# An RWKV-7, neighbourhood-attention and FFN layer: the last merge block behind the last output, weight conversions behind ScalarE's carry copies, and three smaller reorderings

## The chip, the cores and the metric

The kernel runs on one core of one Trainium2 chip, in one launch. The metric is the device time of one execution in microseconds (us). The matrix products run on TensorE (PE, its weight loads PEld), elementwise work on VectorE (DVE) and ScalarE (ACT), some of it and some DMA issues on GpSimd (POOL), and most DMA issues on SyncE (SP). Each engine works through its own queue in order.

## The reference, cut to what matters

One layer is applied to 512 latent tokens and, with the same weights, to 128 context tokens; the kernel works on all 640 columns at once.

```python
def _trunk_layer(x, cvec, s0, ctx_k, ctx_v, p):
    sh1, sc1, g1, sh2, sc2, g2 = _modulation(cvec, p["w_ada"], p["b_ada"])
    h = _rmsnorm(x, p["norm1_g"]) * (1.0 + sc1) + sh1
    u_rw, u_na, gate_rw, gate_na = jnp.split(h @ p["w_in"], IN_SPLITS, axis=-1)
    o_rw, s_new = _rwkv_branch(u_rw, s0, ...)
    ...
    o_na = _na_context(q, k, v)      # or _na_latent(...)
    merged = (jax.nn.sigmoid(gate_rw) * (o_rw @ p["w_o_rwkv"])
              + jax.nn.sigmoid(gate_na) * (o_na @ p["w_o_na"]))
    x = x + g1 * (merged @ p["w_out"])
    h2 = _rmsnorm(x, p["norm2_g"]) * (1.0 + sc2) + sh2
    x = x + g2 * ((jax.nn.silu(h2 @ p["ffn_w1"]) * (h2 @ p["ffn_w3"])) @ p["ffn_w2"])
    return x, s_new, k, v
```

The RWKV branch has 8 heads of 64. The step that costs most is the scan `s = s*w + (s a) b + v k`, once forward and once backward over the tokens, with `k_bonus = 0.5*(k_dir[0] + k_dir[1])` entering the output through `sum(r * k_bonus * r_k) * v`.

## The kernel before, in words

**Products.** A weight or activation is held as two parts, `hi` (rounded) and `lo` (what is left), and a product is three matmuls: hi by hi, hi by lo, lo by hi (`feat_gen`, L220 to L233). A weight chunk comes by DMA as `wst`; `wcast` (L191) makes both parts: for some chunks ScalarE writes the negated copy (L197), a GpSimd DMA adds the chunk to it (L198) and ScalarE writes the `hi` part (L199); for the others ScalarE writes `hi` and VectorE subtracts (L202). An activation is split by `split` (ScalarE L218, VectorE L219).

**Stages.** Norm, modulation and the QKV products run until about 190 us, the attention until about 240 us. Then come four RWKV blocks, `ct` = 0 to 3, of two heads each, until about 621 us; then the last merge products and the output projection `w_out` until about 660 us; then the second norm and the FFN, to the end.

**One block.** `main` forms the products between the chunks' keys (the first are the matmuls of L1306 on `AG`, which VectorE fills at L1285; `R_` is filled at L1288). `inv` inverts triangular matrices on VectorE alone, from the transpose L1412 to the transposes L1462 and L1464, and TensorE's L1475 waits for them. `carry` then takes the states through eight steps, each a chain between engines: TensorE L1536 forms `px`, ScalarE copies it (`x0`, L1539), TensorE L1565 multiplies, ScalarE copies to `ZV` (L1571), TensorE L1578 multiplies, VectorE scales (L1590). During the carry, `prep` prepares the next block: small products (`lora`, L762 and L764) that ScalarE reads through activations (L767, L770), copies for a second small product (L791, read by TensorE at L796), powers and exponentials (L786, L819 to L838), and products on VectorE (L840 to L868). The last of them, L868, adds the two directions into `bv`, which the bonus product reads later (L1268). `out` normalises the block's result and splits it (`yo`).

**What fills TensorE meanwhile.** A generator `stream` runs the large projections and merge products, in the units that the table `order` lists: `l`, `k`, `r`, `v` and `g` for projections, `a0` to `a3` for the attention part of the merge product, `b0` to `b3` for its RWKV part. Between the steps of the block's own work it issues some of these matmuls into two PSUM tiles (`fl`). Work that other engines do on a finished product (the copies L657 to L663 and the shifts L668 to L671 of a projection, the gates of a merge product, the conversion of a weight) is put off by `later` with a due time counted in TensorE's steps, and with a cost (ScalarE's and VectorE's share in us); a weight's conversion has the cost (1.05, 0). `tick` lets what is due run. In the carry, `beside(gen, budget)` fills each of a step's slots with due work and with steps of `prep` until a budget is used up. Slot 1 stands in front of L1536, slot 2 in front of `x0` and slot 3 behind the `ZV` copies.

**The end of the RWKV stage.** Merge unit `b<i>` covers output tiles `c8` = 2i and 2i + 1, each in two halves of 320 columns. Nine matmuls a half take the three finished blocks (a tile of `o` each). VectorE then multiplies the product by the gate (L1708, tile `mx`) and adds it to `mt` (L1710): eight instructions for a unit. The fourth block's result, `o3`, is there only after the last `out`. `last_gen` (L1834 to L1846) therefore forms its part for all eight `c8` in 16 half-steps: three matmuls (L1840) into one of three PSUM tiles, gate times product (L1841) and sum (L1843) on VectorE, the `hi` part `mh` on ScalarE (L1844), and the `lo` part `ml` on GpSimd (L1845). Of the first matmuls of `w_out` (L318), which read `mh` and `ml`, the table `lw` places two behind each of the last 11 half-steps.

Of the kernel before, what the change touches and what calls it, by code (L numbers as in the profile page):

```python
# [14 lines left out]
P = 128  # L15
# [13 lines left out]
     "a3 b0 b1 b2 b3"),  # L29
# [27 lines left out]
    lw=(0, 0, 0, 0, 0, 2, 2, 2, 2, 2, 2, 2, 2, 2, 2, 2),  # L57
# [59 lines left out]
def body(ctx: ExitStack, tc: tile.TileContext, xs, xp, cols, consts, w_ada, b_row, w_rw, w_qkv,  # L117
# [103 lines left out]
    def feat_gen(ps, chunk, act_hl, nk, t0, t1, width=128, wcol=0, k0=0):  # L221
# [429 lines left out]
    def proj_gen(ci, out, ps_, usb, utag, ubufs, w):  # L651
# [23 lines left out]
        later(lambda: shift(512, 640, 514), (0.4, 0.8), 2)  # L675
# [174 lines left out]
    def prep_bk(ct, S, d):  # L850
# [361 lines left out]


    with ExitStack() as s3:
# [386 lines left out]
        def out(ct, S):  # L1601
# [18 lines left out]
            for hf in range(2):  # L1620
# [55 lines left out]
        def merge_cast(g, i, w, eng):  # L1676
            if g == "b" and not i:
                gate_load()
# [4 lines left out]
        def gate_load():  # L1683

            if len(gates) < 8:
                gates.append(sb.tile([P, NT], F32, tag="mx", bufs=2, name=nm("mx")))
                sp.dma_start(gates[-1], trw_d[len(gates) - 1])

        def merge_gen(g, i, w):

            k0, nk = (0, 4) if g == "a" else (4, 3)
            for j in range(2):
# [3 lines left out]
                for (a, b) in halves:  # L1696
                    ps = wps() if (g, i) == ("b", 3) else flps()
# [4 lines left out]
                    def rest(a=a, b=b, ps=ps, c8=c8):  # L1702
# [4 lines left out]
                        t = gates[c8]  # L1707
# [32 lines left out]
        def weave(gen, others=(), bud=None):  # L1740

            for _ in (_ for g in ((0,), gen, (0,)) for _ in g):
# [22 lines left out]
        with tc.manual_schedule(engines=FIRST):  # L1765
# [4 lines left out]
            for ct in range(4):  # L1770
# [32 lines left out]
                def last():  # L1803
# [4 lines left out]
                    if ct < 3:  # L1808
# [15 lines left out]
            need(*(f"b{i}" for i in range(4)))  # L1824
# [4 lines left out]
    mh, ml = hilo("m")  # L1829
    def last_gen():  # L1830
        ts_ = []
        for c8 in range(8):
            t = pre_t() if c8 < 4 else trp.tile([P, NT], F32, tag="tr", bufs=4, name=nm("tr"))
            sp.dma_start(t, trw_d[c8])  # L1834
            ts_.append(t)
        for c8, t in enumerate(ts_):
            for (a, b) in halves:
                ps = pp.tile([P, 512], F32, tag="tp", name=nm("fl"))
                for n, (w, x) in enumerate(((wo[0], o3[0]), (wo[0], o3[1]), (wo[1], o3[0]))):
                    pe.matmul(ps[:, :H2], w[:, c8 * 128:c8 * 128 + 128], x[:, a:b], start=n == 0, stop=n == 2)  # L1840
# [695 lines left out]
```

## Time and profile before

| | us |
|---|---|
| median of three runs | 1121.64 |
| the three runs | 1120.66, 1121.64, 1124.62 |
| the profiled execution, its own time | 1120.04 |
| its span | 1118.3 |

The page gives each engine's busy time over the span, and the trace tells, for each instruction, when it started and what ended the wait in front of it. A wait counts for the time only where TensorE, or the chain that feeds it, stands in it. Matmuls overlap, and their ends are modelled: a 128x320 matmul is listed with about 0.31 us and the next one starts 0.147 us behind it. So this text measures TensorE's losses from start to start, and a gap that a row gives in brackets is a lower bound of the loss. Between the span and the execution's own time lie 1.7 us, which the change does not touch.

### The profile page before, as it was taken

What the parts mean: (1) busy time and instruction counts of PE and PEld (TensorE: products, weight loads), DVE (VectorE), ACT (ScalarE), POOL (GpSimd) and SP (SyncE); (2) the same over time, 40 slices, a digit from 0 to 9 for tenths busy, and PEclk for the clock granted to TensorE, in tenths of its full rate; (3) what the DMA queues carried; (4) which work ended last, traced back from release to release, by engine and by line L of the source; (5) the groups of instructions that cost most, each with busy time, mean ns of one, the idle gap of its engine ahead of it and who ended that gap; (6) DMA issues with size and microseconds to landing.
All of it is one profiled execution on the core that took longest, in us unless ns stands there. A gap on an engine that the chain in (4) does not pass through costs nothing.

```text
span 1118.3 us, 27121 instructions
## 1 busy us (share of the span) xinstructions
PE 1092.3 (98%) x11118; PEld 969.3 (87%) x11118; DVE 813.8 (73%) x1709; ACT 571.4 (51%) x1110; POOL 244.8 (22%) x318
## 2 busy tenths in 40 slices
PE   6999999999999999999999999999999999999998
PEld 4788878799888988888998788998999989989987
DVE  4655465769648947945887946989888887889854
ACT  4544566665575665566453525554544544444430
POOL 1163254320101212110100521242113012131100
PEclk9999999999999999999999999999999999999999
DMA  9853787655423443343734783387567566675622
GB/s 342 297 87 102 216 279 237 203 155 132 109 64 102 113 126 96 99 122 95 285 98 130 232 266 116 126 198 186 150 169 172 151 161 175 171 170 144 159 76 95
DMA packets 72995, 179.05 MB, mean 160 GB/s; under 512 B 8708, under 2 KB 23684, under 8 KB 72872
## 3 DMA queue, kind: packets, MB, share of 16 engines
q1 hardware_dynamic: 58488, 140.86, 38.2%
q0 software_dynamic: 12368, 33.56, 16.6%
q10 hardware_dynamic: 2016, 2.90, 0.8%
q8 instruction: 87, 1.43, 0.5%
q14 instruction: 36, 0.29, 0.1%
HBM read 137.81 MB, written 16.94 MB: 138 GB/s over the span
## 4 chain that ended last, share of the span: by engine, by line
PE 75%; DVE 11%; issue 7%; ACT 5%; DMA 2%; POOL 1%; SPq 0%; ACTq 0%; DVEq 0%; POOLq 0%
PE f L2065 21%; PE acc L318 15%; PE fl L230 10%; PE y L2326 9%; PE mm L230 5%; PE lg L1076 1%; PE pt L1105 1%; PE po L1123 1%; DVE pr L1443 1%; DVE RL L1447 1%; PE psa L1161 1%; DMA wa<-in_w_ada_dram 1%; PE w L1565 1%; DVE wlo L2113 1%; PE fl L704 1%
## 5 line engine op out<-in xcount | busy, mean ns | idle before, releaser
L2065 PE MATMUL f<-t,whi 128*128 128x320 f32 x640 | 141.7, 309 | 0.6 <-ACT whi L2110 0.4
L2065 PE MATMUL f<-b,whi 128*128 128x320 f32 x608 | 135.0, 310 | 0.4 <-DVE b L219 0.4
L230 PE MATMUL fl<-h,whi 128*128 128x320 f32 x672 | 122.6, 321 | 0.9 <-ACT U L657 0.7
L2065 PEld LDWEIGHTS f<-t,whi 128*128 128x128 f32 x640 | 106.9, 188 | 1.2 <-ACT whi L2110 0.7
L230 PEld LDWEIGHTS fl<-h,whi 128*128 128x128 f32 x672 | 101.2, 188 | 6.5 <-ACT U L657 0.9
L2065 PEld LDWEIGHTS f<-b,whi 128*128 128x128 f32 x608 | 101.8, 188 | 1.2 <-issue 0.6
L2065 PE MATMUL f<-t,wlo 128*128 128x320 f32 x320 | 99.0, 309 | 0.2 <-DVE wlo L2113 0.2
L2065 PE MATMUL f<-b,wlo 128*128 128x320 f32 x304 | 94.0, 309 | 0.1
L199 ACT CAST whi<-wst 128x1024 fp32r<-128x1024 f32 (+1 forms) x64 | 66.0, 1031 | 35.4 <-DMA wst<-in_w_out_dram 20.5
L2110 ACT CAST whi<-ws 128x1024 fp32r<-128x1024 f32 x40 | 42.1, 1052 | 68.7 <-PE f L2065 40.3
L318 PE MATMUL acc<-whi,h 128*128 128x512 f32 x240 | 75.6, 396 | 1.5 <-ACT h L453 1.5
L198 POOL DMA_DIRECT2D wlo<-wst x28 | 24.9, 890 | 177.4 <-ACT wlo L197 145.3
L230 PE MATMUL fl<-h,wlo 128*128 128x320 f32 x336 | 62.3, 317 | 0.0
L2065 PEld LDWEIGHTS f<-t,wlo 128*128 128x128 f32 x320 | 60.1, 188 | 0.5 <-DVE wlo L2113 0.5
L202 DVE TENSOR_TENSOR wlo<-wst,whi 128x1024 fp32r<-128x1024 f32 (+2 forms) x44 | 44.7, 1027 | 21.0 <-ACT whi L199 20.3
L2065 PEld LDWEIGHTS f<-b,wlo 128*128 128x128 f32 x304 | 57.1, 188 | 0.4 <-DVE wlo L2113 0.4
L2124 POOL TENSOR_TENSOR ws<-wst 128x512 f32<-128x512 f32 x20 | 30.5, 1526 | 121.5 <-DVE wlo L2113 90.7
L2113 DVE TENSOR_TENSOR wlo<-ws,whi 128x1024 fp32r<-128x1024 f32 x40 | 53.5, 1337 | 4.2 <-ACT whi L2110 4.2
L318 PEld LDWEIGHTS acc<-whi,h 128*128 128x128 f32 x240 | 44.2, 188 | 11.8 <-ACT h L453 2.0
L1590 DVE TENSOR_TENSOR ZV<-w,Dt 64x128 f32<-64x128 f32 x64 | 18.5, 289 | 48.4 <-PE w L1578 47.2
L230 PEld LDWEIGHTS fl<-h,wlo 128*128 128x128 f32 x336 | 51.1, 188 | 1.8
L1099 POOL TENSOR_TENSOR L<-L,m 128x384 f32<-128x384 f32 (+1 forms) x40 | 32.1, 824 | 93.0 <-DVE m L1098 74.9
(388 smaller groups left out, 2823.3 us busy)
## 6 DMA issues: line engine op xcount, KB each, us to landing
wst<-in_w_dram SPq DMA_DIRECT2D x58, 512.0 KB
wst<-in_w_rw_dram SPq DMA_DIRECT2D x31, 512.0 KB
wlo<-wst POOLq DMA_DIRECT2D x28, 512.0 KB, 4.6
wa<-in_w_ada_dram SPq DMA_DIRECT2D x22, 512.0 KB
f<-in_w_ada_dram SPq DMA_DIRECT2D x18, 512.0 KB
t<-in_w_dram SPq DMA_DIRECT2D x16, 512.0 KB
wst<-in_w_qkv_dram SPq DMA_DIRECT2D x12, 512.0 KB
o<-o_d SPq DMA_DIRECT2D x14, 320.0 KB
```

The source lines that it names most:

```text
L198: pool.dma_start(lo[:, :n].bitcast(F32), st[:, :n], accum_op=ALU.add)
L199: act.copy(hi[:, :n], st[:, :n])
L202: dve.tensor_tensor(out=lo[:, a:b], in0=st[:, a:b], in1=hi[:, a:b].bitcast(F32), op=ALU.subtract)
L230: pe.matmul(ps[:, :t1 - t0], w[:, a:a + 128], x[:, k0 + kt, t0:t1], start=n == 0, stop=n == 3 * nk - 1)
L318: pe.matmul(pss[i][:, a:b], lhs(x, kt, ts_), w[:, cs_], start=ki == 0 and n == 0, stop=ki == last and n == 2)
L1099: pool.tensor_tensor(out=L, in0=L, in1=V(m[:, :], [[0, w]], 3), op=ALU.mult)
L1590: dve.tensor_tensor(out=V(ZV[own, l + 1, h, :], [[128 * dl, 2], [1, 64]]), in0=V(pn[own, :], [[64, 2], [1, 64]], 64 * g), in1=V(Dt[own, 0, ...
L2065: pe.matmul(ps[:, :H2], w_[:, c_], x_[:, kt, :], start=first and kt + n == 0, stop=last and kt == 3 and n == 2, skip_group_check=more)
L2110: act.copy(r[0][:, :width], src())
L2113: dve.tensor_tensor(out=r[1][:, :width], in0=src(), in1=r[0][:, :width].bitcast(F32), op=ALU.subtract)
L2124: eng_x(PRM["se"][i - 1]).tensor_tensor(out=o_, in0=x, in1=y, op=op)
L2326: pe.matmul(ps(b), lhs(kind, xh, fs, p, tp), U[k][p][wh][:, half * 512:half * 512 + 512], start=b not in started, stop=True, skip_group_ch ...
```

## The change

**The merge.** `order` takes `b0` behind `b3`. Its four halves (`c8` 0 and 1) are accumulated in four PSUM tiles that stay open (`more` in `feat_gen`); when the last `out` is done, three matmuls a half add `o3`'s part on top (`last_step`, called by `finish`). The separate gate and sum of these halves are gone, so eight VectorE instructions fewer. `last_gen` has 12 half-steps left, for `c8` 2 to 7, each followed by three matmuls of `w_out` (`lw`). The `lo` part `ml` is formed by VectorE, two half-steps behind (`lows`). The gate rows of `c8` 0 and 1 are loaded early.

**The bonus sum.** L868 of block 1 is issued behind the `AG` and `R_` products instead of ahead of them.

**The conversions.** In blocks 0 to 2 `beside` takes no weight conversion into slot 2, so that it falls into slot 3. Five conversions move behind the `ZV` copies: one in block 0, two in block 1, two in block 2; what the budget of slot 2 then still allows are steps of `prep`, some of which come one slot earlier.

**Two smaller moves.** In the `out` of block 1 a `tick(6)` lets the copy L657 of projection `k2` go ahead of the first `yo` cast (L218). The 128-column shift of projection `k1` (L669, L671) gets a due time of 8 steps instead of 2 and goes behind the second bonus product (L1276) of block 0.

```diff
-     "a3 b0 b1 b2 b3"),
+     "a3 b1 b2 b3 b0"),
...
-    lw=(0, 0, 0, 0, 0, 2, 2, 2, 2, 2, 2, 2, 2, 2, 2, 2),
+    lw=(3, 3, 3, 3, 3, 3, 3, 3, 3, 3, 3, 3),
...
-    def feat_gen(ps, chunk, act_hl, nk, t0, t1, width=128, wcol=0, k0=0):
+    def feat_gen(ps, chunk, act_hl, nk, t0, t1, width=128, wcol=0, k0=0, more=False):
...
-                              start=n == 0, stop=n == 3 * nk - 1)
+                              start=n == 0, stop=n == 3 * nk - 1 and not more)
...
-    def beside(gen, budget):
+    def beside(gen, budget, casts=True):
...
-            if pend and pend[0][0] <= 0:
+            if pend and pend[0][0] <= 0 and (casts or pend[0][1] != (1.05, 0)):
...
-        later(lambda: shift(512, 640, 514), (0.4, 0.8), 2)
+        later(lambda: shift(512, 640, 514), (0.4, 0.8), 8 if ci == 5 else 2)
...
-            eng.tensor_tensor(out=S.bv, in0=S.bv, in1=V(NK[:, 1, :], [[-1, 640]], 639), op=ALU.add)
-            yield 0, 0.8 if eng is dve else 0
+            S.bonus = lambda: eng.tensor_tensor(out=S.bv, in0=S.bv, in1=V(NK[:, 1, :], [[-1, 640]], 639), op=ALU.add)
+            if ct != 1:
+                S.bonus()
+                yield 0, 0.8 if eng is dve else 0
...
+    def last_step(c8, a, b, ps=None):
...
+        t, first = lt[c8], ps is None
+        if first:
+            ps = pp.tile([P, 512], F32, tag="tp", name=nm("fl"))
+        for n, (w, x) in enumerate(((wo[0], o3[0]), (wo[0], o3[1]), (wo[1], o3[0]))):
+            pe.matmul(ps[:, :H2], w[:, c8 * 128:c8 * 128 + 128], x[:, a:b], start=first and n == 0, stop=n == 2)
+        dve.scalar_tensor_tensor(out=t[:, a:b], in0=t[:, a:b], scalar=1.0, in1=ps[:, :H2],
+                                 op0=ALU.add, op1=ALU.mult)
+        dve.tensor_tensor(out=t[:, a:b], in0=mt[c8][:, a:b], in1=t[:, a:b], op=ALU.add)
+        act.copy(mh[:, c8, a:b], t[:, a:b])
+        lows.append(lambda: dve.tensor_tensor(out=ml[:, c8, a:b], in0=t[:, a:b], in1=mh[:, c8, a:b].bitcast(F32),
+                                              op=ALU.subtract))
+        if len(lows) > 2:
+            lows.pop(0)()
...
+                if ct == 1 and not hf:
+                    tick(6)
...
+                    if g == "b" and not i:
+                        ps = wps()
+                        yield from feat_gen(ps, w, o, nk, a, b, wcol=j * nk * 128, k0=k0, more=True)
+                        if ready[0]:
+                            finish()
+                        held.append((c8, a, b, ps))
+                        continue
...
-                            beside(o_, bud[n - 1])
+                            beside(o_, bud[n - 1], n == 1 or ct == 3)
...
+                        if ct == 0:
+                            S2.bonus()
...
-            need(*(f"b{i}" for i in range(4)))
+            need("b1", "b2", "b3")
+            ready[0] = True
+            need("b0")
+            finish()
```

Where this moves instructions is shown at three places, each first as the kernel before has it and then as the changed kernel does. In the changed kernel the lines from 1285 on are higher by 26 and more (its L1311, L1314, L1438, L1565 and L1597 are the L1285, L1288, L1412, L1539 and L1571 of before), lines 1231 to 1235 lie in `last_step`, and most tile numbers differ by a little.

ScalarE in block 1's carry, around `x_792` (the step that prepares block 2); `wst_5238` is the weight chunk that is converted, `pre_5374` what TensorE's L796 reads. Before:

```order
L197 ACTIVATE wlo_5397<-wst_5238 128x1024
L199 CAST whi_5396<-wst_5238 128x1024
L767 ACTIVATE pre_5410<-w_5412,D 128x320
L1539 COPY x_792_5425<-w_5416 128x256
L1571 COPY ZV<-w_5452 64x2x64 x4
L767 ACTIVATE pre_5410<-w_5472,D 128x320
L767 ACTIVATE pre_5411<-w_5476,D 128x320
L767 ACTIVATE pre_5411<-w_5480,D 128x320
L791 COPY pre_5374<-r_787_5407 128x320 x2
```

After:

```order
L767 ACTIVATE pre_5405<-w_5407,D 128x320
L767 ACTIVATE pre_5405<-w_5411,D 128x320
L767 ACTIVATE pre_5406<-w_5415,D 128x320
L1565 COPY x_792_5428<-w_5419 128x256
L1597 COPY ZV<-w_5455 64x2x64 x4
L197 ACTIVATE wlo_5476<-wst_5238 128x1024
L199 CAST whi_5475<-wst_5238 128x1024
L767 ACTIVATE pre_5406<-w_5480,D 128x320
L791 COPY pre_5374<-r_785_5402 128x320 x2
```

The conversion stands behind the four `ZV` copies instead of ahead of `x_792`, three L767 instead of one stand ahead of `x_792`, and between the `ZV` copies and the two copies to `pre_5374` stand now the conversion and one L767.

VectorE between blocks 0 and 1, where the next block's `AG` is filled. Before:

```order
L859 TENSOR_TENSOR f_694_4350<-NK_4345,pre_4067 128x10x64
L868 TENSOR_TENSOR bv_4342<-bv_4342,NK_4345 128x640
L1285 TENSOR_TENSOR AG<-kk_3998,P_653_4043 64x10x64 x2
L1285 TENSOR_TENSOR AG<-kk_3998,P_674_4185 64x10x64 x2
L1288 TENSOR_TENSOR R__2906<-rt__630,P_653_4043 128x640
L1288 TENSOR_TENSOR R__2906<-rt__630,P_674_4185 128x640
L1412 STREAM_TRANSPOSE RL_4538<-Nt 128x1024
```

After:

```order
L859 TENSOR_TENSOR f_692_4345<-NK_4340,pre_4067 128x10x64
L1311 TENSOR_TENSOR AG<-kk_3998,P_653_4043 64x10x64 x2
L1311 TENSOR_TENSOR AG<-kk_3998,P_674_4185 64x10x64 x2
L1314 TENSOR_TENSOR R__2906<-rt__630,P_653_4043 128x640
L1314 TENSOR_TENSOR R__2906<-rt__630,P_674_4185 128x640
L868 TENSOR_TENSOR bv_4337<-bv_4337,NK_4340 128x640
L1438 STREAM_TRANSPOSE RL_4538<-Nt 128x1024
```

The sum of `bv` has gone from in front of the four `AG` products to behind the two `R_` products, in front of the transpose that opens the inversion.

VectorE at the end of the last `out`, from the split of `o3` (L219) on. Before, with the four halves of `c8` 6 and 7 and the first of the half-steps:

```order
L219 TENSOR_TENSOR o_1180_9025<-out_8936,o_1179_9024 128x320 x2
L1708 SCALAR_TENSOR_TENSOR mx_8991<-mx_8991,w_9005 128x320
L1710 TENSOR_TENSOR kk_8294<-kk_8294,mx_8991 128x320
L1708 SCALAR_TENSOR_TENSOR mx_8991<-mx_8991,w_9028 128x320
L1710 TENSOR_TENSOR kk_8294<-kk_8294,mx_8991 128x320
L1708 SCALAR_TENSOR_TENSOR mx_9038<-mx_9038,w_9054 128x320
L1710 TENSOR_TENSOR bv_8431<-bv_8431,mx_9038 128x320
L1708 SCALAR_TENSOR_TENSOR mx_9038<-mx_9038,w_9066 128x320
L1710 TENSOR_TENSOR bv_8431<-bv_8431,mx_9038 128x320
L1841 SCALAR_TENSOR_TENSOR pre_9102<-pre_9102,fl_9118 128x320
L1843 TENSOR_TENSOR pre_9102<-mt_7739,pre_9102 128x320
```

After, with the four held halves of `c8` 0 and 1 and the first half-step for `c8` 2:

```order
L219 TENSOR_TENSOR o_1181_9027<-out_8940,o_1180_9026 128x320 x2
L1231 SCALAR_TENSOR_TENSOR pre_8931<-pre_8931,w_9007 128x320
L1233 TENSOR_TENSOR pre_8931<-mt_7739,pre_8931 128x320
L1231 SCALAR_TENSOR_TENSOR pre_8931<-pre_8931,w_9030 128x320
L1233 TENSOR_TENSOR pre_8931<-mt_7739,pre_8931 128x320
L1231 SCALAR_TENSOR_TENSOR pre_8933<-pre_8933,w_9060 128x320
L1233 TENSOR_TENSOR pre_8933<-mt_7842,pre_8933 128x320
L1235 TENSOR_TENSOR m_9053<-pre_8931,m_9052 128x320
L1231 SCALAR_TENSOR_TENSOR pre_8933<-pre_8933,w_9076 128x320
L1233 TENSOR_TENSOR pre_8933<-mt_7842,pre_8933 128x320
L1235 TENSOR_TENSOR m_9053<-pre_8931,m_9052 128x320
L1231 SCALAR_TENSOR_TENSOR pre_9120<-pre_9120,fl_9132 128x320
```

The eight gate and sum instructions on `mx` (two halves each of `kk` and `bv` as `mt`) are gone from there; a `lo` part (`m_9053`) stands behind each step from the third on.

## Rows read from the trace of the kernel before

**Rows 1.** The page's first part: busy us (share of the span) xinstructions.

```profile
PE 1092.3 (98%) x11118; PEld 969.3 (87%) x11118; DVE 813.8 (73%) x1709; ACT 571.4 (51%) x1110; POOL 244.8 (22%) x318
```

**Rows 2.** Windows, start:end, length, busy us of each engine, granted clock, DMA share, GB/s.

```profile
622.00:643.00 21.00, 19.79 (x103) 15.39 (x103) 20.25 (x40) 13.05 (x21) 13.77 (x14) 1.00 0.77 220
...
660.00:1118.30 458.30, 452.48 (x2693) 420.47 (x2691) 371.26 (x539) 202.72 (x294) 86.21 (x83) 1.00 0.57 155
```

**Rows 3.** Timeline, TensorE, blocks 0 to 1: start, us, instruction, [idle before <-releaser].

```profile
339.50 1.44 PE L1306 MATMUL w<-AG,f 64*32 64x64 f32 x122 [0.56 <-DVE AG L1285]
```

**Rows 4.** Timeline, VectorE, blocks 0 to 1.

```profile
335.34 0.81 DVE L868 TENSOR_TENSOR bv<-bv,NK 128x640 f32<-128x640 f32 x1
336.08 3.37 DVE L1285 TENSOR_TENSOR AG<-kk,P 64x640 f32<-64x640 f32 x4
...
343.80 1.25 DVE L1412 STREAM_TRANSPOSE RL<-Nt 128x1024 f32<-128x1024 f32 x1 [2.76 <-ACT Nt L1311]
```

**Rows 5.** Timeline, ScalarE, block 1, behind `x_792`.

```profile
394.03 0.86 ACT L1571 COPY ZV<-w 64x128 f32<-64x128 f32 x4 [1.17 <-PE w L1565]
395.53 1.36 ACT L767 ACTIVATE pre<-w,D 128x320 f32<-128x320 f32 x3 [0.64 <-PE w L764]
396.77 0.82 ACT L791 COPY pre<-r 128x320 f32<-128x320 f32 x2
```

**Rows 6.** Timeline, TensorE, block 1, at `x_792`.

```profile
393.35 0.63 PE L1565 MATMUL w<-x,Rt 64*64 64x64 f32 x16
...
397.75 0.71 PE L796 MATMUL w<-K,pre 128*128 128x128 f32 x5
```

**Rows 7.** Timeline, ScalarE, block 1, around `x_824`.

```profile
407.41 1.07 ACT L197 ACTIVATE wlo<-wst 128x1024 fp32r<-128x1024 f32 x1
...
409.29 0.28 ACT L1539 COPY x<-w 128x128 f32<-128x128 f32 x1
410.12 0.54 ACT L1571 COPY ZV<-w 64x128 f32<-64x128 f32 x2 [0.55 <-PE w L1565]
410.69 0.83 ACT L819 ACTIVATE P<-pre 128x320 f32<-128x320 f32 x2
...
413.61 0.27 ACT L1539 COPY x<-w 128x128 f32<-128x128 f32 x1
```

**Rows 8.** Timeline, TensorE: bonus of block 0; block 1; its end and inversion; block 2.

```profile
260.71 0.28 PE L1330 MATMUL w<-R__2906,f 64*64 64x64 f32 x3 [0.67 <-DVE bv L1276]
...
409.63 0.45 PE L1565 MATMUL w<-x,Rt 64*64 64x64 f32 x8 [0.51 <-ACT x L1539]
...
459.81 0.85 PE L230 MATMUL fl<-h,whi 128*128 128x320 f32 x4 [0.67 <-ACT U L657]
...
470.90 0.83 PE L1475 MATMUL w<-f,Nt 32*32 32x32 f32 x39
...
507.88 0.45 PE L1565 MATMUL w<-x,Rt 64*64 64x64 f32 x8 [0.39 <-ACT x L1539]
```

**Rows 9.** Timeline, VectorE, the end of block 2's inversion.

```profile
470.63 1.22 DVE L1464 STREAM_TRANSPOSE f<-RL 128x1024 f32<-128x1024 f32 x1
```

**Rows 10.** Timeline, TensorE, the last merge products and `w_out`.

```profile
625.19 1.48 PE L1840 MATMUL fl<-o,f 128*128 128x320 f32 x9
...
640.36 2.46 PE L318 MATMUL acc<-wlo,m 128*128 128x512 f32 x10
```

**Rows 11.** Timeline, VectorE, the last merge products.

```profile
623.22 0.48 DVE L1708 SCALAR_TENSOR_TENSOR mx<-mx,w 128x320 f32<-128x320 f32 x1
...
626.91 0.48 DVE L1841 SCALAR_TENSOR_TENSOR pre<-pre,fl 128x320 f32<-128x320 f32 x1
...
629.27 0.65 DVE L1843 TENSOR_TENSOR pre<-mt,pre 128x320 f32<-128x320 f32 x1
```

**Rows 12.** Timeline, GpSimd, the last merge products.

```profile
628.49 8.67 POOL L1845 TENSOR_TENSOR m<-pre,m 128x320 fp32r<-128x320 f32 x8 [0.36 <-ACT m L1844]
```

**Rows 13.** Groups by line and shape, 625.1 to 640.5: busy us, mean ns, idle before.

```profile
L1840 PE MATMUL fl<-o,f 128*128 128x320 f32 x48 | 10.5, 333 | 1.2 <-DVE pre L1841 1.2
```

More of the change, by code (lines that the diff above doesn't have):

```diff
@@ L1211, in body, with last_t @@
             gtag.pop()
+    mh, ml, lt, lows = Two([]), Two([]), {}, []
+    def last_t(c8, t):
+        lt[c8] = t
+        sp.dma_start(t, trw_d[c8])
+    def last_step(c8, a, b, ps=None):
+        if not mh.ts:
+            for q, t in enumerate((mh, ml)):
+                t.ts.append(hp_t("m", q, 0))
+        t, first = lt[c8], ps is None
[11 more added lines that the diff above has]
+            lows.pop(0)()
     with ExitStack() as s3:
@@ L1676, in merge_cast @@
         def merge_cast(g, i, w, eng):
+            if g == "b" and i == 1:
+                gate_load()
             if g == "b" and not i:
-                gate_load()
+                for c8 in range(2):
+                    last_t(c8, pre_t())
             return wcast(w, eng)
@@ L1683, in gate_load, with finish @@
         def gate_load():
-            if len(gates) < 8:
+            if len(gates) < 6:
                 gates.append(sb.tile([P, NT], F32, tag="mx", bufs=2, name=nm("mx")))
-                sp.dma_start(gates[-1], trw_d[len(gates) - 1])
+                sp.dma_start(gates[-1], trw_d[len(gates) + 1])
+        held, ready = [], [False]
+        def finish():
+            while held:
+                last_step(*held.pop(0))
         def merge_gen(g, i, w):
@@ L1696, in merge_gen @@
                 for (a, b) in halves:
-                    ps = wps() if (g, i) == ("b", 3) else flps()
+                    if g == "b" and not i:
[5 more added lines that the diff above has]
+                        continue
+                    ps = flps()
                     if a and g == "b":
@@ L1706, in rest @@
                             return
-                        t = gates[c8]
+                        t = gates[c8 - 2]
                         dve.scalar_tensor_tensor(out=t[:, a:b], in0=t[:, a:b], scalar=1.0, in1=ps[:, :b - a],
@@ L1823, in body @@
             c0 = wload(w_out[0], pool)
-            need(*(f"b{i}" for i in range(4)))
+            need("b1", "b2", "b3")
+            ready[0] = True
+            need("b0")
+            finish()
     pp = open_pool(ctx, "pp4", bufs=3, space=PSUM)
-    mh, ml = hilo("m")
+    for q, t in enumerate((mh, ml)):
+        t.ts.extend(hp_t("m", q, j) for j in range(1, 4))
     def last_gen():
[L1831 to L1836, printed above, removed]
-            for (a, b) in halves:
-                ps = pp.tile([P, 512], F32, tag="tp", name=nm("fl"))
-                for n, (w, x) in enumerate(((wo[0], o3[0]), (wo[0], o3[1]), (wo[1], o3[0]))):
-                    pe.matmul(ps[:, :H2], w[:, c8 * 128:c8 * 128 + 128], x[:, a:b], start=n == 0, stop=n == 2)
-                dve.scalar_tensor_tensor(out=t[:, a:b], in0=t[:, a:b], scalar=1.0, in1=ps[:, :H2],
-                                         op0=ALU.add, op1=ALU.mult)
-                dve.tensor_tensor(out=t[:, a:b], in0=mt[c8][:, a:b], in1=t[:, a:b], op=ALU.add)
-                act.copy(mh[:, c8, a:b], t[:, a:b])
-                pool.tensor_tensor(out=ml[:, c8, a:b], in0=t[:, a:b], in1=mh[:, c8, a:b].bitcast(F32),
-                                   op=ALU.subtract)
+        for c8 in range(2, 8):
+            last_t(c8, pre_t() if c8 < 4 else trp.tile([P, NT], F32, tag="tr", bufs=4, name=nm("tr")))
+        for c8 in range(2, 8):
+            for (a, b) in halves:
+                last_step(c8, a, b)
+                if (c8, b) == (7, NT):
+                    while lows:
+                        lows.pop(0)()
                 yield
```

## The prediction, as it was put on record

> **What bounds the kernel now.** I read the page's busy shares first: TensorE is busy 98% of the span, VectorE 73%, ScalarE 51% [rows 1]. Only a loss on TensorE, or in a chain that it waits for, can be won back. Second, the windows: behind 660 us TensorE is busy 452.48 of 458.30 us at a granted clock of 1.00 [rows 2]. Nothing of the change lies there, so what is won before 660 us stays won, and what is lost stays lost. Third, the timeline at the places that the change touches, TensorE first and then the engine that it waits for. The reader should see two kinds of places: the block's own chain, where TensorE waits for one ScalarE copy or one VectorE product [rows 3, 8], and the stretch from 625 to 640 us, where VectorE feeds TensorE step by step [rows 10, 11].
>
> **The baseline.** Durations are from the profiled execution, whose own time was 1120.04 us; the median of the runs is 1121.64, with 1120.66 and 1124.62 beside it. The sum is a difference, and I apply it to the median.
>
> **A, the bonus sum and block 0's conversion.** The sum L868 takes the place from 335.34 to 336.08, 0.74 us, in front of the four `AG` products, which take 3.37 us together [rows 4]. TensorE's L1306 waits for the third and the fourth of them, 0.56 us for the last by the idle column, and its last group starts at 339.50, when the fourth is done [rows 3]. With L868 behind the `R_` products all four are done 0.74 earlier, and that group starts at about 338.76. The moved sum costs nothing: VectorE waits 2.76 us in front of the transpose at 343.80 [rows 4], more than its 0.81. The wait for `AG` does not vanish, since VectorE still makes a product in 0.85 us. The conversion that leaves slot 2 in block 0 has no idle time listed behind it; from start to start it can hold back its step by a few tenths at most. With it I take **-0.9** (-0.75 to -0.95).
>
> **B, block 1, `x_792`.** Here the conversion was free: TensorE runs L1565 at 393.35 without a gap in front [rows 6]. Behind the `ZV` copies it is not. These start at 394.03 and take 0.86, the L767 behind them 0.45 each, the two copies L791 0.82 [rows 5]; a conversion takes 1.88, the time from L197 at 407.41 to the copy behind it at 409.29 [rows 7]. In the new order four more lora matmuls, 0.147 each (worked out under H), stand in front, so that the `ZV` copies end at 394.89 + 0.59 = 395.48; adding 1.88, 0.45 and 0.82, L791 ends at 398.6. TensorE's L796, which reads it, stood at 397.75 [rows 6], and nothing may overtake it on TensorE. That is a new wait of **+0.9**; +0.45 if the first matmul needs only the first of the two copies.
>
> **C, block 1, `x_824`.** Here the conversion was in the way: L1565 at 409.63 has 0.51 us of idle time, 0.7 from start to start, put down to the copy `x` [rows 8]. That is won first. But from the `ZV` copies at 410.12 to the next copy at 413.61 ScalarE has no gap [rows 7]: 0.57 for the copies, 0.86 for the two exponentials L819 and 2.06 for the rest. The conversion now stands in that stretch, and the exponentials, shorter by a us, in front of it. The `ZV` copies come 0.7 earlier, at 409.4; with 0.57, the conversion's 1.88 and the 2.06, the next copy comes at 413.9 instead of 413.61. So the next step is late by **+0.3** against before, where I would otherwise have counted -0.7.
>
> **D and E, block 2.** The step at `x_983` repeats C: 0.39 us of idle time at 507.88 [rows 8], 0.6 by starts, is won and lost again in the next copy, **+0.4** by the same working. The one at `x_942` repeats B without the harm, since its L796 comes far enough behind; **-0.1** (0 to -0.2).
>
> **F and G, the two smaller moves.** Before 459.81 TensorE waits 0.67 us for the copy of `U`, and before 260.71 0.67 for the second bonus product [rows 8]. Both waits go. But both lie in an inversion, whose end TensorE awaits: VectorE is at the last transposes when L1475 starts, at 470.90, with L1464 begun at 470.63 [rows 8, 9], and the same pair stands in block 0. TensorE arrives earlier and waits longer there. **-0.1** for F and **0** for G; together -1.7 if the inversion were not the bound, no loss on the other side.
>
> **H, the last merge products.** From 625.19 to 640.36 TensorE issues 48 matmuls of L1840 and 22 of L318 [rows 10, 13]. A 128x320 is 0.147 us behind the last, (1.48 - 0.31)/8, a 128x512 is 0.229, (2.46 - 0.40)/9 [rows 10]. Without a wait they take 48 x 0.147 + 22 x 0.229 = 12.1 us, so 15.17 - 12.1 = 3.1 us are lost. The cause is VectorE: it is still at the eight gate and sum instructions from 623.22 to 626.91, 0.92 us a pair [rows 11], and while GpSimd subtracts (eight in 8.67 us, [rows 12]) the sum takes 0.65 instead of 0.49, and a pair 1.08.
> After the change 36 matmuls of L318 stand in the stretch. Measured to the same work, before ends at 640.36 + 14 x 0.229 = 643.6. After the change TensorE has 18 matmuls of the held halves, 48 of L1230 and 36 of L318 from 2.65 us ahead of 625.19 on: 2.65 + 7.06 + 8.24, done at 640.5 if nothing waits. What waits: the first `o3` product for the `lo` part that VectorE is only then making (0.3), the first `w_out` matmul for the first `ml` (0.55), and the steps: VectorE now has three instructions a step, 0.92 + 0.41 = 1.33 us, against TensorE's 3 x 0.147 + 3 x 0.229 = 1.13. It falls behind by 0.2 a step over 12 steps, of which four steps done ahead and three PSUM tiles take up all but some 0.5. The end is then 641.9, **-1.7**; the bounds are -3.1 (no wait) and -0.9 (0.3, 0.55 and the full 2.4 less one step's lead of 1.1).
>
> By the idle column alone this term would be sized otherwise: it shows 1.2 us in front of L1840 [rows 13]. The Trainium skill, "Perfetto Trace Analysis", section "Identifying the Most-Contended Engine", says that matmul busy time is a bad measure because matmuls are pipelined, and wants the weight loads' busy share instead. Here that share is 15.39 of 21.00 us, 73%, against 87% over the span [rows 1, 2], which makes 2.9 us lost: the trace agrees with the rule, and with the 3.1. Had I gone by the column, the new waits of 1.4 would outweigh the 1.2, and the sum below would be +0.7.
>
> **The sum.** -0.9 + 0.9 + 0.3 - 0.1 + 0.4 - 0.1 + 0 - 1.7 = -1.2 us. **1121.6 - 1.2 = 1120.4 us.** The edits on ScalarE, B to E, together cost 1.5 and eat A.
>
> **The rivals.**
> *R1: each removed wait counts and none comes in its place.* 0.95 (A), 0.7 (C), 0.6 (E), 0.8 and 0.9 (F, G, from start to start) and 3.1 (H) make -7.1: **1114.5**. For it speaks that TensorE is the bound nearly everywhere. Against it: the transposes at 470.63 end just ahead of L1475 [rows 9], ScalarE's stretch to 413.61 is full [rows 7], and VectorE's step stays longer than TensorE's.
> *R2: VectorE becomes the bound of the last stretch.* The `lo` parts wait for ScalarE's `mh` casts, and these stand in order with conversions of 0.94 each. With a step of VectorE of 1.33, the stretch ends 1.7 early; each tenth of a us more costs 12 x 0.1 = 1.2, so that it breaks even at about 1.5 us a step. If each step waits 0.42 for ScalarE, less than half a conversion, it is 1.75 us, 12 x 0.25 = +3.0 beyond that, and with +0.5 from the other terms the kernel is slower by 3.5: **1125.1**. For it: GpSimd no longer helps, and a pair took up to 1.08 already. Against: what took it from 0.92 to 1.08 was GpSimd's own subtraction, which is gone.
> *R3: the end stretch does not do what it says.* The three matmuls a step fill TensorE but the first `ml` comes late, and only the moves A to G remain: +0.5, **1122.1**.
> *R4: the conversions find a gap.* If B waits for one copy only and C and E cost nothing net, the sum is -2.5: **1119.1**.
>
> **How the numbers follow.** My forecast, with R4 beside it as its own lower part, has 0.67 (0.52 and 0.15), R3 0.12, R2 0.11, R1 0.10. The forecast's terms reach from -3.4 (H at -3.1, B at +0.45) to +0.1 (H at -0.9, A at -0.75 and D at 0), and the runs of before lie 4 us apart; from 1115.5 to 1124.0 covers these, R3, R4 and the milder half of R2, and leaves out R1. About 0.5%, 5.6 us, is what a measurement of this kernel can tell from no change. Faster by more than that, under 1116.0, needs R1: 0.09. Slower by more, over 1127.2, is beyond R2's price: 0.02. Between them 0.89.
>
> **What would show it.** A: the last L1306 group begins 0.75 earlier against the conversion ahead of it, with one wait for `AG` left. B: a new wait for `pre` of L791 in front of L796 in block 1. C and E: no gap at the step's own L1565, but a late copy `x` in the next one. F and G: no wait for `U` and `bv`, and L1475 waits longer for the transposes. H: weight loads in the last stretch at 80% instead of 73%, no GpSimd subtraction, sums at 0.49 throughout, and the same 36 matmuls of `w_out` done about 1.7 us earlier. I am wrong if L1475 has no wait in front of it, if L796 doesn't wait, or if a step of VectorE behind 625 us takes over 1.5 us.

## The result, and the profile after

| | median, us | runs |
|---|---|---|
| before | 1121.37 | 22 (1119.62 to 1124.62) |
| changed | 1123.95 | 22 (1121.53 to 1126.28) |
| ratio | 1.0022 | 95%: 1.0016 to 1.0028 |
| forecast | 1120.4 | |

The changed kernel is slower by 2.5 us (1.8 to 3.1), where 1.2 us faster was forecast. The time lies inside the range, and within 0.5% of before, where most of the chance was; the sign is wrong. That it lies inside is luck: the range's upper end, 1124.0, was drawn for the milder half of R2, whose mechanism did not come. The profiled execution took 1124.72 us, 4.7 more than before's; 1.0 of that lies ahead of the first moved instruction (a wait for GpSimd at 231 us that some profiles show and others don't, with and without the change), so the medians are the better measure.

The page's first part of the changed kernel, as in [rows 1]:

```profile
PE 1093.2 (97%) x11118; PEld 971.1 (86%) x11118; DVE 815.2 (73%) x1717; ACT 571.6 (51%) x1110; POOL 228.3 (20%) x302
```

Its windows by stage (columns as in [rows 2]; the last merge products come 5 us later here):

```profile
326.00:425.00 99.00, 92.43 (x1660) 83.30 (x1655) 69.50 (x196) 59.87 (x136) 15.74 (x29) 0.98 0.40 102
...
627.00:648.00 21.00, 20.51 (x113) 17.57 (x112) 18.59 (x43) 15.42 (x25) 4.35 (x5) 1.00 0.88 237
...
660.00:1122.90 462.90, 456.77 (x2710) 423.74 (x2709) 373.64 (x542) 202.78 (x294) 85.71 (x83) 1.00 0.57 154
```

In before the first of these stretches reads:

```profile
326.00:425.00 99.00, 96.36 (x1699) 86.36 (x1698) 73.70 (x203) 63.44 (x145) 17.79 (x30) 1.00 0.39 102
```

From 326 to 425 us TensorE is now idle 6.6 us where it was idle 2.6, and the granted clock is 0.98 in the mean where it was 1.00. The list of what TensorE waited for (total us, times, longest) names the place:

```profile
PE w L1411 <- issue: 3.7, 1, 3.7
PE w L1591 <- ACT x L1565: 2.5, 4, 1.0
...
PE w L1501 <- DVE f L1488: 0.9, 2, 0.5
...
PE w L796 <- ACT pre L791: 0.5, 1, 0.5
```

The three lower rows are waits that the prediction spoke of (E and C, F, B). The first is one that it did not: "issue" is time in which the engine waited for nothing of the program. TensorE's timeline there:

```profile
339.50 1.43 PE L1332 MATMUL w<-AG,f 64*32 64x64 f32 x122 [0.56 <-DVE AG L1311]
...
343.96 0.28 PE L1411 MATMUL w<-K,f 64*64 64x64 f32 x3
347.97 1.02 PE L1411 MATMUL w<-K,f 64*64 64x64 f32 x27 [3.73 <-issue]
```

In before the same group runs as one:

```profile
343.98 0.80 PE L1385 MATMUL w<-K,f 64*64 64x64 f32 x30
```

One group of thirty equal matmuls is torn after the third. No semaphore that the profile shows holds the other 27; what is left, and what the experiments below test, is that TensorE does not have their code yet. The windows around it show the clock: it falls at about 347.8 us (0.94 in the mean until 348), while TensorE still stands, and is 0.50 (1.2 GHz) in place of 1.00 (2.4 GHz) behind the wait:

```profile
344.00:346.00 2.00, 0.24 (x9) 0.10 (x3) 1.97 (x3) 0.54 (x3) 0.75 (x6) 1.00 0.81 162
346.00:348.00 2.00, 0.03 (x4) 0.03 (x4) 1.61 (x10) 0.00 (x0) 0.00 (x0) 0.94 0.04 6
348.00:350.00 2.00, 2.00 (x65) 2.00 (x67) 0.00 (x0) 0.65 (x2) 0.00 (x0) 0.50 0.56 115
350.00:352.00 2.00, 2.00 (x37) 1.88 (x32) 1.35 (x4) 0.52 (x2) 0.00 (x0) 0.71 0.66 233
```

Code comes by DMA too. It is the queue q8 that the page calls "instruction"; 87 packets make 1.43 MB there, 16 KB each. That this queue is TensorE's is read from the counts: 11118 matmuls and as many weight loads over 87 packets make 256 instructions a packet. The DMA view of the kernel before, from 341.7 to 344 us (queue, kind: packets, MB, share of 16 engines), has one of them:

```profile
q1 hardware_dynamic: 53, 0.22, 38.7%
q8 instruction: 1, 0.02, 2.6%
q0 software_dynamic: 1, 0.00, 0.0%
```

The same view of the changed kernel, from 341.7 to 345.5, has none,

```profile
q0 software_dynamic: 126, 0.49, 64.9%
q1 hardware_dynamic: 106, 0.37, 28.8%
```

and from 345.5 to 347 the late one:

```profile
q0 software_dynamic: 16, 0.03, 11.6%
q8 instruction: 1, 0.02, 3.9%
```

By its own record the packet ran from 341.77 to 342.73 before, and from 345.54 to 346.48 now; TensorE goes on 1.5 us behind its end. It starts among the last packets of GpSimd's DMA (q0), the 512 KB transfers by which L198 makes a low part. When they are issued, GpSimd's timeline tells, of before

```profile
329.13 0.85 POOL L198 DMA_DIRECT2D wlo<-wst  x1 [13.70 <-ACT wlo L197]
337.61 0.85 POOL L198 DMA_DIRECT2D wlo<-wst  x1 [7.63 <-ACT wlo L197]
```

and of the changed kernel:

```profile
335.07 0.86 POOL L198 DMA_DIRECT2D wlo<-wst  x1 [18.64 <-ACT wlo L197]
339.08 0.85 POOL L198 DMA_DIRECT2D wlo<-wst  x1 [3.15 <-ACT wlo L197]
```

Block 0's conversion, moved behind the `ZV` copies, comes 6 us later, and its transfer with it, into the stretch that holds two stores, a weight load and the other low part. From 336 to 346 us the DMA engines hardly rest, and the code comes at the end of it.

### The profile page after: what moved, and what is told of

It is laid out like the page before. It is cut to its first block, busy times and chain, and to the rows that moved or that the text cites. A ratio compares the mean times of both kernels' runs of the same rounds, so it can differ in the third digit from the quotient of the medians.

```text
span 1122.9 us, 27096 instructions
## 1 busy us (share of the span) xinstructions
PE 1093.2 (97%) x11118; PEld 971.1 (86%) x11118; DVE 815.2 (73%) x1717; ACT 571.6 (51%) x1110; POOL 228.3 (20%) x302
## 3 DMA queue, kind: packets, MB, share of 16 engines
q8 instruction: 87, 1.43, 0.5%
## 5 line engine op out<-in xcount | busy, mean ns | idle before, releaser
L198 POOL DMA_DIRECT2D wlo<-wst x28 | 24.9, 888 | 190.9 <-ACT wlo L197 169.9
```

Source lines behind the costliest of these rows:

```text
L198: pool.dma_start(lo[:, :n].bitcast(F32), st[:, :n], accum_op=ALU.add)
```

## The experiments

Theory 1 is what the traces suggest: the fetch of TensorE's code follows the transfers, and the moved conversion of block 0 has made it late. Theory 2: that wait is one of a single execution, and the conversions of blocks 1 and 2, which gave the forecast its losses, cost more than they seem to. Theory 3 came for the second set: the fetch is late for a reason of TensorE's own, not for the transfers.

| kernel | median | ratio to before, 95% | code's packet, us | wait of TensorE for it |
|---|---|---|---|---|
| before | 1121.37 | 1 | 341.77 to 342.73 | none |
| changed | 1123.95 | 1.0022 (1.0016 to 1.0028) | 345.54 to 346.48 | 3.73 |
| changed, block 0 back | 1120.99 | 0.9993 (0.9982 to 1.0004) | 344.93 to 345.87 | 1.03 |
| before, block 0's move only | 1124.73 | 1.0035 (1.0021 to 1.0048) | 346.26 to 347.20 | 2.69 |
| changed, all conversions back | 1119.14 | 0.9983 (0.9973 to 0.9994) | 342.58 to 343.56 | 0.94 |
| before, blocks 1 and 2 only | 1123.00 | 1.0013 (1.0005 to 1.0022) | 342.75 to 343.66 | 0.2 |
| changed, a transfer left out | 1119.63 | 0.9983 (0.9974 to 0.9992) | 342.27 to 343.21 | 0.40 |
| before, 512 KB more | 1121.45 | 1.0003 (0.9990 to 1.0017) | 347.88 to 348.81 | 0.78 |
| before, 1 MB more | 1122.69 | 1.0013 (1.0001 to 1.0025) | 343.49 to 344.44 | 1.88 |
| conversions back, low part on VectorE | 1120.12 | 0.9988 (0.9979 to 0.9997) | 341.01 to 341.97 | none |
| before, bonus sum only | 1120.93 | 1.0001 (0.9992 to 1.0010) | 342.99 to 343.91 | 1.04 |
| before, merge only | 1119.01 | 0.9979 (0.9970 to 0.9989) | 341.38 to 342.46 | none |
| before, smaller moves only | 1121.28 | 0.9996 (0.9985 to 1.0006) | 341.31 to 342.28 | none |
| merge and smaller moves | 1120.28 | 0.9987 (0.9977 to 0.9997) | 341.82 to 342.75 | none |

(Each profile has its own offset of up to 5 us from what lies ahead, so a packet's time is compared with the wait beside it, not with another row's. The medians come from four sets of runs, each with its own runs of before; the ratios are to those. "None" is a gap that the row does not list.)

Where a trace is used for a loss, it is counted by matmul: all kernels issue 11118 matmuls, and the start of the n-th in one profile, less its start in before's, says how far TensorE is behind there. Between 343 and 355 us of before, the stretch with the torn group, the changed kernel falls 4.67 us back: the wait of 3.73 and what follows it, the low clock with it. A part of a shorter wait is made up, since TensorE waits behind the group in before as well (0.31 us for `AG` at 348.73).

**Block 0's conversion back, in the changed kernel.**

```diff
-                            beside(o_, bud[n - 1], n == 1 or ct == 3)
+                            beside(o_, bud[n - 1], n == 1 or ct in (0, 3))
```

> The changed kernel, but in block 0 a weight conversion may again stand in slot 2; blocks 1 and 2 stay as changed. Theory 1 (the loss is TensorE's wait of 3.7 us for its own instructions at 344 us, because block 0's conversion, moved, shifts 512 KB transfers into the time in which the instructions are fetched): that wait is gone, and with it the low clock behind it, so about 5 us less than the changed kernel in a profile, and 1.0 us faster than before (1120.4 on a median of 1121.4). Theory 2 (that wait is one of this profile alone; the moves in blocks 1 and 2 cost what the median lost): still 2 to 3 us slower than before.

1120.99: the loss is gone, by 0.0029 of the time, 3.3 us, against the changed kernel. The wait has shrunk to 1.03, not to nothing, and TensorE loses 0.59 us in the stretch instead of 4.67; the bonus sum explains what is left, below. Against theory 2.

**Block 0's move alone, on the kernel before.** `beside` gets its argument `casts`, and:

```diff
-                            beside(o_, bud[n - 1])
+                            beside(o_, bud[n - 1], n == 1 or ct != 0)
```

> The kernel before with one edit: in block 0 no weight conversion in slot 2 (one conversion moves). Theory 1: TensorE waits 2 to 4 us for its instructions near 344 us and runs at the lower clock for some 2 us behind it; 3 to 5 us slower than before. Theory 2: within 0.5 us of before, no such wait.

3.9 us slower (2.4 to 5.4), as theory 1 has it, with the same tear in the same thirty matmuls (TensorE's timeline):

```profile
345.51 0.28 PE L1385 MATMUL w<-K,f 64*64 64x64 f32 x3
348.48 0.63 PE L1385 MATMUL w<-K,f 64*64 64x64 f32 x27 [2.69 <-issue]
```

One moved conversion, 1.9 us of ScalarE with nothing waiting for it, costs this alone. How much is less certain than in the changed kernel: these are five runs, and in the profile TensorE loses 2.25 us in the stretch and had won 0.28 ahead of it, 2.0 in all, less than the interval's lower end. The clock did not fall behind the wait in this profile. That does not make the low clock an accident of one execution: the mean granted clock is below 1.00 in all five of these runs (0.995 to 0.998), and in 21 of the changed kernel's 22, of which the one at 1.000 is the fastest (1121.53); with block 0's conversion back it is 1.000 in 7 of 11.

**All conversions back, in the changed kernel.**

```diff
-                            beside(o_, bud[n - 1], n == 1 or ct == 3)
+                            beside(o_, bud[n - 1])
```

> The changed kernel with all five conversions back in slot 2; the merge at the end, the bonus sum and the two smaller moves stay. Theory 1: no wait for instructions, and none of the losses in blocks 1 and 2 (0.69, 0.54 and 0.66 us), so A's 0.76, the end's 1.9 and 0.15 are left: 2.8 us faster than before (about 1118.6). Theory 2: about the same, 2.5 faster. Would the wait stay, its cause were the bonus sum or another edit: 2 slower.

1.9 us faster than before (0.7 to 3.0) by the ratio, a little less than the 2.8 expected; a wait for code of 0.94 is left, which theory 1 had not foreseen here.

**The moves of blocks 1 and 2 alone, on the kernel before.**

```diff
-                            beside(o_, bud[n - 1])
+                            beside(o_, bud[n - 1], n == 1 or ct in (0, 3))
```

> The kernel before with one edit: in blocks 1 and 2 no weight conversion in slot 2 (four conversions move). Theory 1: a new wait of 0.7 us in front of L796 in block 1, and the two late x0 copies, 0.5 and 0.7 net; 1.7 us slower than before, no wait for instructions at 344 us. Theory 2: 3 to 4 us slower.

1.5 us slower (0.6 to 2.5): the losses that B, C and E named, and no more. With the other run, the five moved conversions together cost some 5 us, of which block 0's one costs most; between the changed kernel and the one with all of them back the ratios differ by 4.4.

**The transfer of block 0's low part left out, in the changed kernel.** The conversion stays where the change put it.

```diff
-            pool.dma_start(lo[:, :n].bitcast(F32), st[:, :n], accum_op=ALU.add)
+            casts_p[0] += 1
+            if casts_p[0] != 8:
+                pool.dma_start(lo[:, :n].bitcast(F32), st[:, :n], accum_op=ALU.add)
```

> The changed kernel, but the 512 KB transfer by which GpSimd adds the chunk to the low part of the conversion that moved in block 0 is left out (that chunk's low part is then wrong); ScalarE's conversion stays where the change put it. Theory 1 (the fetch of TensorE's instructions waits behind the transfers on the DMA engines): the transfers behind it come about 2 us earlier, the fetch starts at 343 to 344 instead of 345.5, TensorE waits 1.5 to 2.3 us instead of 3.7, and the kernel is 1.5 to 2.5 us faster than the changed one. Theory 3 (the conversion itself, or the time at which TensorE comes there, makes the fetch late): the wait stays at 3.7 us.

The wait falls to 0.40, TensorE loses nothing in the stretch, and the kernel is 4.4 us faster than the changed one, more than expected: the transfers behind come earlier too, and the fetch with them.

```profile
344.47 0.63 PE L1415 MATMUL w<-K,f 64*64 64x64 f32 x27 [0.40 <-issue]
```

ScalarE's work is unchanged, so it is the 512 KB and not the conversion that makes the code late; theory 3 falls.

**More traffic, in the kernel before.** `w_rw` chunks are copied to an unused place in HBM, on SyncE's queue behind the weight load of 336 us, once and twice:

```diff
                     ds.append(us[i + 2][1]())
+                    for q in range(1 if i + 2 == 18 else 0):
+                        x = sp.dma_start(xtr[q], w_rw[q])
...
```

> The kernel before with one DMA more, 512 KB from HBM to HBM, on SyncE's queue behind the weight load of about 336 us; nothing else is moved. Theory 1: the low part's transfer ends some 2.3 us later (at about 344.2 instead of 341.9), the fetch starts behind it, TensorE waits some 2.3 us for its instructions; 2 to 4 us slower than before. Theory 3: no such wait, within 0.5 us of before.

> The same with two such DMAs, 1 MB. Theory 1: the wait grows by another 2.3 us, to some 4.6 us; 4.5 to 6.5 us slower than before. Theory 3: within 0.5 us of before.

A wait for code appears where before listed none, 0.78 and 1.88 us, and grows with the traffic. The size expected was over twice that: by the DMA view of before the engines rest for part of 338 to 339.4 us, and a part of the added transfer may go there, which is not shown apart. In time, 0.3 us (-1.1 to +1.9, not to be told from nothing) and 1.5 us (0.1 to 2.8) slower; by the traces TensorE loses 0.35 and 1.45 in the stretch. With 1 MB more, TensorE's row reads

```profile
345.80 0.63 PE L1391 MATMUL w<-K,f 64*64 64x64 f32 x27 [1.88 <-issue]
```

**The low part of k2's chunk on VectorE, with the conversions back.**

```diff
-    wl="dddddddddppppppppppppppppppppppdddpdddd", nu=9, lg=14, jo=(2, 0, 1), cut=((), (), (9, 28), (8,)), na=(
+    wl="dddddddddppppppppdpppppppppppppdddpdddd", nu=9, lg=14, jo=(2, 0, 1), cut=((), (), (9, 28), (8,)), na=(
```

> The changed kernel with the five conversions back in slot 2, and with the low part of the chunk for projection k2 made by VectorE behind the bonus sum, where it waits 2 us, instead of by a 512 KB transfer (the one that the fetch of TensorE's instructions follows at 342.6 there). Theory 1: the fetch starts 2 to 3 us earlier, the 0.9 us that TensorE waits for its instructions at 344 us are gone, and it is 1.0 us faster than with the conversions back alone: about 1118.1, 3.6 less than before. Theory 3: no change against that kernel.

Theory 1's step is right and its price wrong. Without that transfer the code's packet starts at 341.01, at a time when the DMA engines rest (nothing ended in the two us ahead of it), and no wait for code is left. But the kernel is no faster than with the conversions back alone (0.9988 against 0.9983). In its trace TensorE, earlier by 1.4 behind the torn group than with the conversions back, waits 0.76 (from start to start) for `AG` behind 348 and 1.23 in front of L1501 at 472, and the clock falls twice; the mean granted clock is 0.995 to 0.998 in all 11 runs, and 1.000 in 8 of 11 with the conversions back. Its windows:

```profile
350.00:352.00 2.00, 2.00 (x10) 1.66 (x11) 1.23 (x9) 0.00 (x0) 0.91 (x1) 0.72 0.03 8
352.00:354.00 2.00, 2.00 (x59) 1.67 (x61) 2.00 (x12) 0.00 (x0) 1.15 (x3) 0.50 0.00 0
...
474.00:476.00 2.00, 2.00 (x9) 2.00 (x9) 1.99 (x5) 1.90 (x6) 0.00 (x0) 0.50 0.28 61
```

**The bonus sum alone, on the kernel before** (the edit of L868 and of `last` in the change).

> The kernel before with the bonus sum moved, nothing else. Theory 1, extended (the fetch of TensorE's instructions starts behind the low part's transfer, and TensorE cannot get past it): the second wait for AG is gone (0.76), and TensorE waits 0.8 to 1.1 us for its instructions at 344 us instead, so nothing is won: within 0.4 us of before. Rival (what the bonus sum wins stays won): 0.8 us faster.

No gain that can be seen: 0.1 us slower (-0.9 to +1.1). This interval still holds the rival's 0.8 faster, so it is the trace that decides: TensorE is 0.73 us earlier at 341 us, and 0.61 of that is lost in the stretch with the torn group. TensorE's timeline shows both halves, the one wait for `AG` where there were two, and the wait for code that takes the gain:

```profile
339.56 1.43 PE L1308 MATMUL w<-AG,f 64*32 64x64 f32 x122 [0.56 <-DVE AG L1287]
...
345.35 0.63 PE L1387 MATMUL w<-K,f 64*64 64x64 f32 x27 [1.04 <-issue]
```

This explains the waits of about 1 us with block 0's conversion back: TensorE reaches the torn group sooner, and the code does not come sooner.

**The merge alone, on the kernel before** (`order`, `lw`, `more`, `last_step` and what calls them).

> The kernel before with the changed merge at the end, nothing else. By the traces: 1.9 us faster than before (1.5 to 2.3), all of it between 620 and 645 us. Rival (part of the gain of the kernel with the conversions back came from the smaller moves): 1.2 or less.

2.4 us faster (1.2 to 3.4): the lowest median here, by the ratios 4.8 us below the changed one, though the kernels with the conversions back and with the transfer left out lie within its interval. By its own trace TensorE gains 1.7 us between 620 and 645 us, which leaves nothing for the rival to explain.

**The two smaller moves alone.**

> The kernel before with the two smaller moves (the tick and the shift's due time), nothing else. Both waits (0.88 and 0.83 from start to start) are gone and come back in front of the inversions' ends: within 0.4 us of before. Rival (they stay won): 1.7 us faster. A second rival (the longer wait in front of L1475 makes the granted clock fall): 1 us slower.

0.4 us faster (1.7 faster to 0.7 slower): not to be told from nothing. The wait for the bonus product is gone, and TensorE waits in front of L1475 instead; behind it the clock falls to 0.50 for some us. The row, and the window that follows it:

```profile
282.16 1.47 PE L1475 MATMUL w<-f,Nt 32*32 32x32 f32 x80 [0.99 <-DVE f L1462]
```

```profile
284.00:286.00 2.00, 2.00 (x10) 2.00 (x9) 2.00 (x4) 1.90 (x5) 0.00 (x0) 0.57 0.00 0
```

By 293 us TensorE is where it would have been: the low clock costs nothing there, probably since the next block's carry waits for other engines, which was not tried.

**The merge and the smaller moves, without the bonus sum.**

> The changed kernel with the conversions back in slot 2 and the bonus sum back in its place: the merge and the two smaller moves. If the bonus sum is worth nothing beside the fetch, this is as fast as with it, 1119.0 to 1119.6 on a median of 1121.5 before; if the bonus sum is worth its 0.76, it is 0.8 slower than with it.

1120.28, ratio 0.9987 against 0.9983 with the bonus sum. The ratios lie 0.5 us apart and the intervals overlap: it does not settle what the bonus sum is worth, and neither does its own run. By the traces 0.13 to 0.24 of its 0.73 us are kept, in the kernels with block 0's conversion back, with all conversions back and with the bonus sum alone.

## Why the prediction was wrong, step by step

**The step that failed is A**, twice. First, the conversion that leaves slot 2 in block 0: the prediction read its idle time and priced it at "a few tenths at most" of gain. That gain came (0.28 by the trace). But it read ScalarE's two instructions and not the 512 KB transfer that goes with them, and so put at nothing what that transfer makes late. Measured, this move costs 3.3 us in the changed kernel, and 3.9 (2.4 to 5.4) alone. The transfer's place in the DMA engines' time had no row in the prediction, and the "instruction" queue was read on the page as a total, not by time. The view that was needed is there in the kernel before: a code packet right behind a low part's transfer (341.77, when the last of the packets of that queue ended at 341.78), and TensorE at the place of the tear: the fourth of the thirty starts at 344.16, 0.12 behind the third and 1.4 behind the packet's end. In all fourteen profiles the fourth starts 1.3 to 1.5 us behind that end, so there was no slack to spend.

Second, the bonus sum: the second wait for `AG` went, as forecast (0.73 for 0.75), but most of the gain counted on TensorE was taken by the same code packet. Worth -0.75 in the sum, and by its own run nothing that can be seen (-0.9 to +1.1).

**B** was right in mechanism and size: a new wait of 0.53 us by the row, 0.69 from start to start, in front of the first of the five matmuls, and 0.2 more among them (0.90 for the 0.71 of [rows 6]): 0.9 in all. ScalarE's order did what the working said:

```profile
400.14 1.06 ACT L197 ACTIVATE wlo<-wst 128x1024 fp32r<-128x1024 f32 x1
...
402.59 0.80 ACT L791 COPY pre<-r 128x320 f32<-128x320 f32 x2
```

```profile
403.09 0.90 PE L796 MATMUL w<-K,pre 128*128 128x128 f32 x5 [0.53 <-ACT pre L791]
```

**C and E** were right: the wait at the step's own L1565 [rows 8] is gone, worth 0.74 and 0.62, and the next one is late, 1.26 us from start to start where it had been about 0.22. So +0.3 and +0.4 net, as forecast.

```profile
419.76 0.45 PE L1591 MATMUL w<-x,Rt 64*64 64x64 f32 x8 [1.05 <-ACT x L1565]
```

B, C, D and E together were put at +1.5; alone they measured +1.5 (0.6 to 2.5), and in the changed kernel's trace they make +1.4.

**F and G** were right in size: both waits went, and L1475 (now L1501) waits for the inversion instead [rows 8, 9]. At G's place, 261 us, code comes in as well: TensorE waits there 0.19 us put down to "issue" in the changed kernel, 0.62 with the conversions back, 1.2 to 1.4 behind the end of a code packet.

```profile
476.61 1.10 PE L1501 MATMUL w<-f,Nt 32*32 32x32 f32 x57 [0.52 <-DVE f L1488]
```

**H** was right. VectorE's step is 1.32 us, as the sum had it at 1.33 (from one L1231 to the next), the sums take 0.49 where [rows 11] had 0.65, and GpSimd subtracts nothing:

```profile
634.35 0.48 DVE L1231 SCALAR_TENSOR_TENSOR pre<-pre,w 128x320 f32<-128x320 f32 x1
634.86 0.49 DVE L1233 TENSOR_TENSOR pre<-mt,pre 128x320 f32<-128x320 f32 x1
635.27 0.49 DVE L1235 TENSOR_TENSOR m<-pre,m 128x320 fp32r<-128x320 f32 x1
635.67 0.48 DVE L1231 SCALAR_TENSOR_TENSOR pre<-pre,fl 128x320 f32<-128x320 f32 x1
```

TensorE waits once for the first low part, 0.39 by the row:

```profile
634.49 0.74 PE L318 MATMUL acc<-whi,m 128*128 128x512 f32 x2 [0.39 <-DVE m L1235]
```

Measured to the same `w_out` matmul behind it, TensorE gains 1.9 us in the changed kernel's trace and 1.7 in that of the merge alone, whose runs are 2.4 faster (1.2 to 3.4), for 1.7 forecast. Weight loads fill 17.57 of 21.00 us there, 84% for the 80% expected, where [rows 2] has 73%.

**The rivals.** R1 did not come: each wait removed on TensorE came back, but for the end. R2, slower by VectorE's step in the last stretch, named nearly the time that came, 1125.1, with a mechanism that did not: the step stayed at 1.32. A time that fits is no proof. R3 fell with H, R4 with B, C and E.

**The sum again**, counted by matmul in the profile of the changed kernel against that of before:

| from, to (us in before) | term | forecast | measured |
|---|---|---|---|
| 240, 320 | G | 0 | 0.00 |
| 320, 341 | A, on VectorE and ScalarE | -0.9 | -1.02 |
| 343, 355 | none: the code packet | 0 | +4.67 |
| 390, 405 | B | +0.9 | +0.90 |
| 405, 425 | C | +0.3 | +0.28 |
| 455, 475 | F | -0.1 | -0.10 |
| 475, 515 | D and E | +0.3 | +0.18 |
| 620, 645 | H | -1.7 | -1.93 |
| all | | -1.2 | +2.98 |

Every term that the prediction named came within 0.25 us; the one that it did not name turned the sign. The runs say 2.5 (1.8 to 3.1). Three side sums of the prediction are a little off by its own terms: R4 makes -2.35 and not -2.5, and the forecast's terms reach from -3.05 to -0.15 and not from -3.4 to +0.1. Nothing above rests on them.

## What to carry to other kernels

An engine's own code is a transfer like the others: where a kernel without loops streams its code while weights stream too, look in the DMA view for the code queue by time, and treat each packet as a due time that a gain on TensorE does not move and a transfer in front of it can. Here one packet of 87 was followed closely. A conversion that is moved on ScalarE takes its DMA along; price both. And a gain on TensorE ahead of a packet, or of a chain on another engine that is already late, is worth little until that is moved too.

## What the runs showed of the hardware that was not expected

TensorE's code comes in packets of 16 KB; the one followed here took 0.9 to 1.1 us, and it is held up by data: in before, in the kernels with the conversions back, with the bonus sum, with the merge, with the smaller moves, and with both, the packet starts within 0.02 us of the end of GpSimd's 512 KB transfer (341.77 and 341.78, 342.58 and 342.60, 342.99 and 342.99, 341.38 and 341.39). In the changed kernel and five more it starts 0.3 to 2.3 us before that transfer's last packet ends, with the moves of blocks 1 and 2 alone 0.3 us behind that end, and without such a transfer after 2 us of rest. So which data packet it waits for is not shown; that more data makes it later and less data earlier is. TensorE goes on 1.3 to 1.5 us behind the packet's end in all eight profiles with a wait of 0.4 or more. The Trainium skill, "Runtime: NRT & Kernel Launch", section "Instruction fetch mechanics", has engines fetch code in 16 KiB blocks through a DMA queue of their own while the current one runs, and calls the cost of a block mostly hidden. The packets here agree in size; the cost does not, with 3.73 us in one wait.

The granted clock fell to 0.50 for 3.4 us after some waits of TensorE and not after others. It fell 0.2 us before the end of the 3.73 in the changed kernel, 2.1 us behind the 0.99 in the one with the smaller moves, 1.7 behind a 1.00 at the same place in the one with the merge as well, and 2.6 and 2.0 behind waits of 0.60 and 1.07 in the one with the low part on VectorE; it did not fall behind the 2.69 in the one with block 0's move alone, nor behind a 0.79 in front of the same L1501 with the conversions back. What decides it was not tried. That the clock fell after the small waits of three kernels which took waits away elsewhere is one more reason why those gained little, but not one that these runs measure apart.
